# Delta keys kept unnormalised in a hybrid decoder layer: the norm moves into beta and the values

## The chip, the cores and the metric

The kernel runs on one core of one Trainium2 chip. The metric is the device time of one execution in microseconds (us); the time of a kernel is the median of its runs. Engines are named as in the profile: PE is TensorE (matmul), PEld its loading of weights, DVE VectorE, ACT ScalarE, POOL GpSimd, SP SyncE, on whose queue all transfers here are issued.

## The reference

One decoder layer with 512 tokens (T) and 2048 channels (D): a sliding-window attention branch and a gated DeltaNet branch run side by side on the same normalised input, and a gated sum of both goes through an output projection. What matters here is the delta branch. Its keys, per head of 128 channels, are convolved, passed through SiLU, and divided by their norm:

```python
dq = jnp.repeat(l2_norm(dq.reshape(B, T, DN_K_HEADS, DN_HEAD_K)), rep, axis=2)
dk = jnp.repeat(l2_norm(dk.reshape(B, T, DN_K_HEADS, DN_HEAD_K)), rep, axis=2)
beta = jax.nn.sigmoid(db.astype(f32))
...
k_beta = k * beta[..., None]
v_beta = v * beta[..., None]
L = jnp.where(strict, jnp.einsum('bhncd,bhnsd->bhncs', k_beta, k) * decay, 0.0)
t_inv = lax.linalg.triangular_solve(eye + L, jnp.broadcast_to(eye, L.shape),
                                    left_side=True, lower=True, unit_diagonal=True)
u = t_inv @ v_beta
w = t_inv @ (k_beta * jnp.exp(g)[..., None])
```

There are 16 key heads and 32 value heads; two value heads share a key head. Chunks have 64 tokens. A scan over chunks then uses k, u, w and the decays.

## The kernel before

**Products.** Every large product is computed in fp32 precision by three passes: a weight is split into a high part (whi, a cast on ACT, L61) and a low part (wlo, a subtraction on DVE, L62), and `mm3` (L270 to L275) issues whi with hh, whi with hl, and wlo with hh, where hh and hl are the split activations. A `channel_tile` (L290 to L303) makes 128 output channels for all 512 tokens: 16 steps of three 128x512 matmuls, 48 in all, called products in this document. The weights come in loads of 1 MB ("raw", L215) on SP, two of them held at a time, and are split in halves of 1024 columns, three of which are held.

**Order of the work.** The channel tiles follow each other without a pause, and all other work is woven in between. After every second step of a tile, that is after six products, `pump()` advances the side work: each generator that is alive (`go`) counts down and runs to its next `yield n`, which makes it sleep n pumps; the triangular solve is paced by a budget for each pump (`paced`, 0.36), and another sideline runs at a rate of its own. That gives the order in which the program is written. When it is built, a scheduler orders the instructions of each engine once more by its own idea of when each becomes ready, so a change of a few pumps can shift neighbours on every engine. On the chip each engine then keeps its fixed order.

**Stages.** After the startup come the keys (`delta_keys`, about 125 to 445 us of the profile: 16 key tiles mixed with merge gates), the attention (to about 1015 us: four groups of eight tiles, each opened by the transposition pss, L1418, with scores S, L1451, the softmax tile sm, its transposition pP, L320, the output O, L1514, and a sum of squares qss, L1412), the heads (`delta_heads`, to about 2130 us: 16 groups of five tiles q, v, v, z, z), then the output products of the delta branch and the end of the layer.

**keys()** (L729 to L772) is the side work of one key tile: convolution (`conv`), ptk (four 128x128 transpositions on PE to token order, in one PSUM bank of `ptp`, which has two), the sums of squares (ACT, L778), after three pumps the loads of the decay rows E on SP (L783) and the inverse root rk on DVE (L69 to L74), after four more k = ptk · rk as four activations on ACT (L745) and the masks on E (POOL, L788), after four more ptkT (four transpositions back, of the normalised k) with its copy to kT (ACT, L753), the store of k and eight exponentials on E (ACT, L794), after two more pkk = kT · kT (four matmuls), the store of kT and the product of E and pkk (DVE, L763), and after two more the stores of E to lt_d and lab_d.

**solve()** (L796 to L848) waits for eight key tiles, loads the 64 x 64 triangles and beta, multiplies the triangles by −beta (nbet, L815), inverts them step by step on DVE (L823 and L831, each step a product and a sum of up to 128x1024) and multiplies the inverse by beta. It runs twice, the first time in the keys and attention stages, the second beside the heads.

**heads**: `queries()` (L883 and on) loads kT and k, the decays and the inverses, transposes q (ptq), and makes the chunk matrices; `neg_beta` scales one block of them. `values()` (L866 to L878) convolves v, transposes it (ptv) and copies it to vt (ACT, L877). `scan()` walks four blocks of 128 tokens: it multiplies k and kT with the state S, makes pv and pod, and ends with ms (L1023), an inverse root (L69 to L74, tiles roy and rot), the scaled output osb (L1030), its transposition pto, and its product with the gate z.

Of the kernel before, what the change touches and what calls it, by code (L numbers as in the profile page):

```python
# [45 lines left out]
class Layer:  # L46
# [524 lines left out]
    def gates(self, sp):  # L571

        nc, a, dnc = self.nc, self.a, self.dnc
        pt = self.ptp
        bd = sp.tile([P, NTB, 2 * VH], F32, name="bd")
        S = [P, NTB, VH]
# [11 lines left out]
        nc.vector.tensor_tensor(out=bd, in0=pb[:, :, 2 * VH :], in1=bd, op=ALU.add)  # L588
        beta = self.beta = dnc.tile(S, F32, name="beta")
        e = sp.tile(S, F32, name="ge")  # L590
# [138 lines left out]
    def keys(self, wk, g, ps):  # L729

        nc = self.nc
        y = wk.tile([P, T], F32, tag="y", name="y", bufs=3)
        yield from self.conv(wk, ps, 16 + g, y)
        yield 2
        pt = self.ptp.tile([P, T], F32, tag="tp", name="ptk")
        self.transpose4(pt, lambda c: y[:, c * P : (c + 1) * P])
        ss = self.sumsq(wk, pt)
        yield 3
        E = [self.decay_load(wk, 2 * g + e) for e in range(2)]
        nc.vector.tensor_scalar(out=ss, in0=ss, scalar1=EPS, scalar2=None, op0=ALU.add)  # L740
        rk = self.rsqrt(wk, ss, NTB, "rk")
        yield 4
        k = wk.tile([P, NTB, P], F32, tag="k", name="k")
        for c in range(NTB):
            nc.scalar.activation(k[:, c, :], pt[:, c * P : (c + 1) * P], AF.Copy, scale=rk[:, c : c + 1])  # L745
        for e in range(2):
            self.decay_mask(E[e])
        yield 4
        pt = self.ptp.tile([P, T], F32, tag="tp", name="ptkT")
        self.transpose4(pt, lambda c: k[:, c, :])  # L750
        nc.sync.dma_start(out=self.k_d[g], in_=k.rearrange("p c d -> p (c d)"))
        kT = wk.tile([P, T], F32, tag="kT", name="kT")
        nc.scalar.copy(out=kT, in_=pt)  # L753
        for e in range(2):
# [3 lines left out]
        for c in range(NTB):  # L758
            sl = slice(c * P, (c + 1) * P)
            nc.tensor.matmul(pk[:, c, :], lhsT=kT[:, sl], rhs=kT[:, sl], start=True, stop=True)  # L760
        nc.sync.dma_start(out=self.kT_d[g], in_=kT)
        for e in range(2):
# [33 lines left out]
    def solve(self, wk, b, eng):  # L796
# [16 lines left out]
        nb = wk.tile([P, HD], F32, tag="nbet", name="nbet", bufs=1)  # L813
        self.behind(eng.tensor_scalar(out=nb, in0=bet, scalar1=-1.0, scalar2=None, op0=ALU.mult))
# [54 lines left out]
    def values(self, wk, g, e, ps, st):  # L869
# [6 lines left out]
        vt = wk.tile([P, NTB, P], F32, tag="vt", name="vt", bufs=3)  # L876
        nc.scalar.copy(out=vt.rearrange("p c d -> p (c d)"), in_=pt)  # L877
        st[f"v{e}"] = vt  # L878
# [928 lines left out]
```

## Time and profile before

| what | us |
|---|---|
| three runs | 2845.51, 2839.72, 2842.66 |
| their median | 2842.66 |
| span of the profiled execution, first to last instruction | 2839.0 |
| PE busy in it | 2806.5 |
| PE busy of 175.00 in the keys' first part (125 to 300) | 173.21 |
| PE busy of 145.00 in their second part (300 to 445) | 145.00 |
| PE busy of 570.00 in the attention (445 to 1015) | 567.64 |
| PE busy of 435.00 in the heads' first part (1015 to 1450) | 430.19 |
| PE busy of 680.00 in the heads' second part (1450 to 2130) | 679.69 |

The profiled execution's own time is not listed apart; its span lies 3.7 us below the median of the runs. In the rows of a timeline a duration runs to the modelled end of a pipelined matmul, so the next one starts before it; what an instruction costs PE is read from one start to the next. A row "A <- B" in the waits says that A's engine stood until B had ended. In the rows of groups the numbers behind the bar are the busy us, the mean ns of one instruction, and the idle time before them with what ended it. In a table of windows each engine has its busy us and number of instructions, in the order PE, PEld, DVE, ACT, POOL, and then come the granted clock of TensorE as a share of full speed, the busy share of the DMA engines, and GB/s.

### The profile page before, as it was taken

How to read it: one execution, taken by the hardware profiler on the slowest of the kernel's cores; microseconds unless marked ns; L12 is line 12 of the kernel's file. 1: busy time of each engine (PE TensorE's matmuls, PEld its weight loads, DVE VectorE, ACT ScalarE, POOL GpSimd, SP SyncE). 2: the span in 40 equal slices, each digit the busy share in tenths (PEclk: the TensorE clock that was granted, in tenths of full speed). 3: DMA queues.
4: the chain of work that ended last, by engine and by line, in shares of the span. 5: the costliest groups of instructions: out<-in, count | busy, mean ns of one | idle time of the engine just before them, and what ended most of it. 6: DMA issues, size and time to landing. Idle time of an engine off the chain costs nothing.

```text
span 2839.0 us, 38354 instructions
## 1 busy us (share of the span) xinstructions
PE 2806.5 (99%) x14152; PEld 2283.3 (80%) x14152; DVE 1944.8 (69%) x3185; ACT 1207.1 (43%) x2476; POOL 146.0 (5%) x124
## 2 busy tenths in 40 slices
PE   8999999999999999999999999999999999999999
PEld 6788888877776788888888888888888888878887
DVE  7866876867758667778766666666656766664676
ACT  5555443244544443333434333333334454432443
POOL 0010000100000010000001000000000000000000
PEclk9999999999999999999999999999999999999999
DMA  9877764322243253356777667677647886885684
GB/s 402 335 246 230 257 218 139 110 91 91 82 135 119 101 168 110 117 201 219 247 255 262 235 224 242 210 239 238 231 167 252 289 314 240 302 273 180 242 318 168
DMA packets 228512, 603.25 MB, mean 212 GB/s; under 512 B 76354, under 2 KB 102594, under 8 KB 188002
## 3 DMA queue, kind: packets, MB, share of 16 engines
q1 hardware_dynamic: 228324, 600.80, 62.1%
q8 instruction: 111, 1.82, 0.3%
q14 instruction: 77, 0.63, 0.1%
HBM read 480.32 MB, written 118.17 MB: 211 GB/s over the span
## 4 chain that ended last, share of the span: by engine, by line
PE 91%; DMA 3%; DVE 3%; ACT 1%; issue 1%; SPq 0%; POOL 0%; DVEq 0%; ACTq 0%; POOLq 0%
PE mm L273 22%; PE mm L275 21%; PE mm L274 21%; PE m L274 5%; PE m L273 5%; PE m L275 5%; PE pod L1000 1%; PE O L1514 1%; PE pv L981 1%; DVE wlo L62 1%; PE pod L999 1%; PE pod L996 1%; PE pp L971 1%; PE S L1451 1%; DMA wa<-in_w_ada_ss 1%
## 5 line engine op out<-in xcount | busy, mean ns | idle before, releaser
L273 PE MATMUL mm<-hh,whi 128*128 128x512 f32 x2784 | 1130.4, 406 | 1.5 <-ACT hh L61 1.5
L275 PE MATMUL mm<-hh,wlo 128*128 128x512 f32 x2784 | 1090.4, 392 | 0.0
L274 PE MATMUL mm<-hl,whi 128*128 128x512 f32 x2784 | 1087.9, 391 | 0.0
L62 DVE TENSOR_TENSOR wlo<-raw,whi 128x1024 fp32r<-128x1024 f32 x516 | 636.9, 1235 | 426.4 <-ACT whi L61 415.4
L61 ACT CAST whi<-raw 128x1024 fp32r<-128x1024 f32 x516 | 541.3, 1050 | 799.9 <-PE mm L274 566.6
L273 PEld LDWEIGHTS mm<-hh,whi 128*128 128x128 f32 x2784 | 524.0, 188 | 117.0 <-issue 14.3
L275 PEld LDWEIGHTS mm<-hh,wlo 128*128 128x128 f32 x2784 | 523.0, 188 | 113.8 <-issue 0.2
L274 PEld LDWEIGHTS mm<-hl,whi 128*128 128x128 f32 x2784 | 524.7, 188 | 100.9 <-issue 1.6
L1246 DVE TENSOR_TENSOR q<-q,q 128x1024 f32<-128x1024 f32 x96 | 124.8, 1300 | 0.0
L794 ACT ACTIVATE E<-E,neg_g 128x128 f32<-128x128 f32 x256 | 81.2, 393 | 92.3 <-POOL E L788 89.6
L831 DVE TENSOR_TENSOR A<-A,atmp 128x62 f32<-128x62 f32 (+30 forms) x124 | 109.5, 883 | 0.6
L823 DVE TENSOR_TENSOR atmp<-A 128x62 f32<-128x62 f32 (+30 forms) x124 | 107.4, 866 | 0.4
L928 POOL TENSOR_TENSOR qe<-qe,yq 128x512 f32<-128x512 f32 x32 | 54.1, 1708 | 923.9 <-DMA qe<-eg_rows 695.9
L1001 ACT COPY osb<-pod 128x256 f32<-128x256 f32 x64 | 23.8, 372 | 152.6 <-PE pod L1000 152.6
L788 POOL TENSOR_SCALAR_AFFINE_SELECT E<-E 128x512 f32<-128x512 f32 x64 | 59.1, 936 | 431.2 <-DMA E<-g_rows 384.5
L983 ACT COPY vn<-pv 128x256 f32<-128x256 f32 x64 | 23.8, 372 | 124.4 <-PE pv L981 124.4
L652 DVE SCALAR_TENSOR_TENSOR yv<-mm,convh,yv 128x511 f32<-128x511 f32 (+2 forms) x96 | 71.2, 742 | 1.1
L988 DVE TENSOR_SCALAR vs<-vn,kd 128x128 f32<-128x128 f32 x96 | 23.1, 283 | 58.3 <-ACT vn L983 58.3
L1482 ACT ACTIVATE sm<-sm,mx,rs 128x128 f32<-128x128 f32 x128 | 61.5, 482 | 3.4 <-DVE mx L1477 2.3
L1011 DVE SCALAR_TENSOR_TENSOR S<-S,egl,pod 128x128 f32<-128x128 f32 x64 | 19.3, 342 | 51.0 <-ACT junk L1004 51.0
L472 DVE SCALAR_TENSOR_TENSOR wa<-wa,silu_cb 128x2048 f32<-128x2048 f32 x22 | 50.1, 2285 | 4.8 <-DMA wa<-in_w_ada_ss 4.8
L657 ACT ACTIVATE th<-yv 128x512 f32<-128x512 f32 x32 | 20.1, 630 | 76.4 <-DVE yv L652 73.7
(444 smaller groups left out, 3678.8 us busy)
## 6 DMA issues: line engine op xcount, KB each, us to landing
raw<-in_w_ch SPq DMA_DIRECT2D x158, 1024.0 KB
wa<-in_w_ada_ss SPq DMA_DIRECT2D x32, 1024.0 KB
q<-in_w_od SPq DMA_DIRECT2D x64, 512.0 KB
g_d<-q SPq DMA_DIRECT2D x64, 512.0 KB
raw<-g_d SPq DMA_DIRECT2D x32, 1024.0 KB
raw<-in_w_od SPq DMA_DIRECT2D x24, 1024.0 KB
gw<-in_w_ada_gate SPq DMA_DIRECT2D x16, 1024.0 KB
E<-g_rows SPq DMA_DIRECT2D x64, 256.0 KB
```

Of the source, the lines that this page charges most:

```text
L61: h = self.nc.scalar.copy(out=hi, in_=src)
L62: l = self.nc.vector.tensor_tensor(out=lo, in0=src, in1=hi.bitcast(F32), op=ALU.subtract)
L273: nc.tensor.matmul(ps, lhsT=wh, rhs=xh, start=first, stop=False)
L274: nc.tensor.matmul(ps, lhsT=wh, rhs=xl, start=False, stop=False)
L275: self.last_mm = nc.tensor.matmul(ps, lhsT=wl, rhs=xh, start=False, stop=last)
L652: nc.vector.scalar_tensor_tensor(out=y[:, s:], in0=ps[:, : T - s], scalar=w[:, j : j + 1], in1=y[:, s:], op0=ALU.mult, op1=ALU.add)
L788: self.last_mask = self.nc.gpsimd.affine_select(out=E, in_=E, pattern=[[0, NTB], [1, P]], compare_op=ALU.is_ge, fill=NEG, base=0, channel_ ...
L794: self.nc.scalar.activation(E[:, c, :], E[:, c, :], AF.Exp, bias=self.neg_g[:, c, h : h + 1])
L823: eng.tensor_tensor(out=t, in0=A[:, m : m + 1, m + 1 :].to_broadcast([P, m, n]), in1=A[:, :m, m : m + 1].to_broadcast([P, m, n]), op=ALU.mult,
L831: self.behind(eng.tensor_tensor(out=A[:, :m, m + 1 :], in0=A[:, :m, m + 1 :], in1=t, op=ALU.add))
L1246: self.behind(nc.vector.tensor_tensor(out=q[f], in0=q[x], in1=q[y], op=ALU.add))
L1482: nc.scalar.activation(t, t, AF.Exp, scale=r[:, h : h + 1], bias=mx[:, h : h + 1], accum_out=den[:, h : h + 1])
```

## The change

With unnormalised keys y, the norm of a token enters twice in L (once by each k). The change keeps y wherever k stood and puts the norm elsewhere: `knorm` = ss · rk (the norm itself, ss being the sum of squares with epsilon, rk its inverse root) scales the values, `inv` = 1/ss scales `neg_beta` and, as rows read back from DRAM, the beta of the solve.

- In `keys()` the convolved y serves as kT: it is stored right behind ptk, and pkk is y · y. The transposition ptkT, the tile kT and its copy are gone. y has four buffers in place of three. k is one copy of 128x512 (ACT) behind the sums of squares in place of four activations with scale rk.
- DVE computes knorm, the reciprocal inv and the scaled neg_beta for each tile. Each eighth tile transposes the inverse sums of eight tiles at once (pinv, 128x64 to 64x128), copies the rows and stores them to `inv_d`.
- From the loads of E to the exponentials there are 2 + 2 pumps in place of 4 + 4.
- `solve()` loads two more small tiles from `inv_d` and multiplies beta by them (128x64).
- `values()` copies ptv by four activations with the scale knorm in place of one copy.

```diff
     def keys(self, wk, g, ps):
...
-        y = wk.tile([P, T], F32, tag="y", name="y", bufs=3)
+        y = wk.tile([P, T], F32, tag="y", name="y", bufs=4)
...
         self.transpose4(pt, lambda c: y[:, c * P : (c + 1) * P])
+        nc.sync.dma_start(out=self.kT_d[g], in_=y)
         ss = self.sumsq(wk, pt)
+        k = wk.tile([P, NTB, P], F32, tag="k", name="k")
+        nc.scalar.copy(out=k.rearrange("p c d -> p (c d)"), in_=pt)
         yield 3
...
         rk = self.rsqrt(wk, ss, NTB, "rk")
-        yield 4
-        k = wk.tile([P, NTB, P], F32, tag="k", name="k")
-        for c in range(NTB):
-            nc.scalar.activation(k[:, c, :], pt[:, c * P : (c + 1) * P], AF.Copy, scale=rk[:, c : c + 1])
+        nc.vector.tensor_tensor(out=self.knorm[:, :, g], in0=ss, in1=rk, op=ALU.mult)
...
+        nc.vector.reciprocal(out=inv, in_=ss.unsqueeze(1).to_broadcast([P, 2, NTB]))
+        nb = self.neg_beta[:, :, 2 * g : 2 * g + 2]
+        nc.vector.tensor_tensor(out=nb, in0=nb, in1=inv.rearrange("p e c -> p c e"), op=ALU.mult)
+        nc.sync.dma_start(out=self.k_d[g], in_=k.rearrange("p c d -> p (c d)"))
+        yield 2
         for e in range(2):
             self.decay_mask(E[e])
-        yield 4
-        pt = self.ptp.tile([P, T], F32, tag="tp", name="ptkT")
-        self.transpose4(pt, lambda c: k[:, c, :])
-        nc.sync.dma_start(out=self.k_d[g], in_=k.rearrange("p c d -> p (c d)"))
-        kT = wk.tile([P, T], F32, tag="kT", name="kT")
-        nc.scalar.copy(out=kT, in_=pt)
+        if g % 8 == 7:
+            pt = self.ptp.tile([P, T], F32, tag="tp", name="pinv")
+            (nc.tensor.transpose(pt[:HD, :P], self.inv[b].rearrange("p h c -> p (h c)"), self.ident))
+            rows = wk.tile([HD, P], F32, tag="invr", name="invr", bufs=1)
+            nc.vector.tensor_copy(out=rows, in_=pt[:HD, :P])
+            half = self.inv_d[16 * b : 16 * b + 16]
+            nc.sync.dma_start(out=half.rearrange("h (c i) -> (h c) i", c=NTB), in_=rows)
+        yield 2
         for e in range(2):
             self.decay_exp(E[e], 2 * g + e)
         yield 2
...
-            nc.tensor.matmul(pk[:, c, :], lhsT=kT[:, sl], rhs=kT[:, sl], start=True, stop=True)
-        nc.sync.dma_start(out=self.kT_d[g], in_=kT)
+            nc.tensor.matmul(pk[:, c, :], lhsT=y[:, sl], rhs=y[:, sl], start=True, stop=True)
...
     def solve(self, wk, b, eng):
...
-            nc.sync.dma_start(
-                out=bet[s],
-                in_=self.b_rows.rearrange("h (c k i) -> k (h c) i", c=4, k=2)[k2, b * HD : (b + 1) * HD, :],
-            )
+            for dst, rows in ((bet, self.b_rows), (nb, self.inv_d)):
+                nc.sync.dma_start(
+                    out=dst[s], in_=rows.rearrange("h (c k i) -> k (h c) i", c=4, k=2)[k2, b * HD : (b + 1) * HD, :]
+                )
         yield 8.0
+        self.behind(eng.tensor_tensor(out=bet, in0=bet, in1=nb, op=ALU.mult))
...
     def values(self, wk, g, e, ps, st):
...
-        nc.scalar.copy(out=vt.rearrange("p c d -> p (c d)"), in_=pt)
+        for c in range(NTB):
+            nc.scalar.activation(vt[:, c, :], pt[:, c * P : (c + 1) * P], AF.Copy, scale=self.knorm[:, c, g : g + 1])
```

The change also moves instructions that it doesn't name. In the fences below each row is one instruction of an engine in its fixed order, with its line, operation, tiles and shape; "x4" stands for four in a row. The lines of the new kernel are up to fifteen higher behind `keys()`.

ACT in the keys stage, around one tile's exponentials (L794), before; th and y are steps of convolutions, whi the weight casts, junk the squares of ptk:

```order
L649 ACTIVATE y<-mm,convh 128x512
L745 ACTIVATE k<-ptk,rky 128x128 x4
L61 CAST whi<-raw 128x1024
L753 COPY kT<-ptkT 128x512
L794 ACTIVATE E<-E,neg_g 128x128 x8
L657 ACTIVATE th<-y 128x512
L61 CAST whi<-raw 128x1024
```

The same engine and stage, now:

```order
L791 ACTIVATE junk,ss<-ptk 128x128 x4
L743 COPY k<-ptk 128x512
L309 ACTIVATE mth<-mm 128x512
L61 CAST whi<-raw 128x1024 x3
L807 ACTIVATE E<-E,neg_g 128x128 x8
L649 ACTIVATE y<-mm,convh 128x512
L61 CAST whi<-raw 128x1024
```

The copy of k stands directly behind the squares, kT's copy is gone, and the exponentials (now L807) stand behind a run of weight casts.

PE in the third attention group, before; mm is a product, S, pP, O and qss belong to the attention:

```order
L275 MATMUL mm<-hh,wlo 128x512
L1451 MATMUL S<-kd_4589,aq 64x192 x3
L320 MATMUL pP<-ident,sm 128x128 x3
L1451 MATMUL S<-kd_4589,aq 64x192 x2
L320 MATMUL pP<-ident,sm 128x128 x5
L1451 MATMUL S<-kd_4589,aq 64x192 x4
L1514 MATMUL O<-pT,vtok_a 64x512
L1451 MATMUL S<-kd_4589,aq 64x192 x2
L1514 MATMUL O<-pT,vtok_a 64x512
L1514 MATMUL O<-pT,vch_4530 64x512 x2
L1451 MATMUL S<-kd_4589,aq 64x192
L1412 MATMUL qss<-qsq,blk 32x128
```

The same transpositions pP, now:

```order
L275 MATMUL mm<-hh,wlo 128x512
L320 MATMUL pP<-ident,sm 128x128
L273 MATMUL mm<-hh,whi 128x512
L320 MATMUL pP<-ident,sm 128x128
L274 MATMUL mm<-hl,whi 128x512
L275 MATMUL mm<-hh,wlo 128x512
L320 MATMUL pP<-ident,sm 128x128
L273 MATMUL mm<-hh,whi 128x512
L320 MATMUL pP<-ident,sm 128x128 x2
L274 MATMUL mm<-hl,whi 128x512
L320 MATMUL pP<-ident,sm 128x128 x3
L275 MATMUL mm<-hh,wlo 128x512
```

Before, the group's S, pP, O and qss follow each other without a product between them; now they stand among products, and the eight pP in five pieces.

DVE in the heads, at the end of the scan that falls into the second window between two ptq (of the three that the prediction speaks of), before; roy and rot are the steps of the inverse root:

```order
L69 TENSOR_SCALAR roy<-ms 128x8
L72 SCALAR_TENSOR_TENSOR rot<-roy 128x8
L73 TENSOR_TENSOR rot<-rot,ms 128x8
L74 SCALAR_TENSOR_TENSOR roy<-rot,roy 128x8
L72 SCALAR_TENSOR_TENSOR rot<-roy 128x8
L73 TENSOR_TENSOR rot<-rot,ms 128x8
L74 SCALAR_TENSOR_TENSOR roy<-rot,roy 128x8
L72 SCALAR_TENSOR_TENSOR rot<-roy 128x8
L73 TENSOR_TENSOR rot<-rot,ms 128x8
L74 SCALAR_TENSOR_TENSOR roy<-rot,roy 128x8
L62 TENSOR_TENSOR wlo<-raw,whi 128x1024
L1030 TENSOR_TENSOR osb<-osb,roy 128x512 x2
```

The last part of the same chain, now:

```order
L652 SCALAR_TENSOR_TENSOR yv<-mm,convh,yv 128x511
L73 TENSOR_TENSOR rot<-rot,ms 128x8
L652 SCALAR_TENSOR_TENSOR yv<-mm,convh,yv 128x510
L74 SCALAR_TENSOR_TENSOR roy<-rot,roy 128x8
L652 SCALAR_TENSOR_TENSOR yv<-mm,convh,yv 128x509
L72 SCALAR_TENSOR_TENSOR rot<-roy 128x8
L845 TENSOR_TENSOR A<-A,atmp 128x38x25
L73 TENSOR_TENSOR rot<-rot,ms 128x8
L659 SCALAR_TENSOR_TENSOR yv<-th,yv 128x512
L74 SCALAR_TENSOR_TENSOR roy<-rot,roy 128x8
L62 TENSOR_TENSOR wlo<-raw,whi 128x1024
L1045 TENSOR_TENSOR osb<-osb,roy 128x512 x2
```

The steps of the inverse root, before in one run, now alternate with steps of a value's convolution (yv) and of the solve (A).

More of the change, by code (lines that the diff above doesn't have):

```diff
@@ L588, in gates @@
         nc.vector.tensor_tensor(out=bd, in0=pb[:, :, 2 * VH :], in1=bd, op=ALU.add)
-        beta = self.beta = dnc.tile(S, F32, name="beta")
+        beta = sp.tile(S, F32, name="beta")
         e = sp.tile(S, F32, name="ge")
@@ L670, in delta_keys @@
         self.k_d = dram.tile([KH, P, T], F32, name="k_d")
+        self.inv_d = dram.tile([VH, T], F32, name="inv_d")
+        self.knorm = self.dnc.tile([P, NTB, KH], F32, name="knorm")
+        self.inv = {}
         self.o_d = dram.tile([VH, P, T], F32, name="o_d")
@@ L741, in keys @@
         rk = self.rsqrt(wk, ss, NTB, "rk")
-        yield 4
-        k = wk.tile([P, NTB, P], F32, tag="k", name="k")
-        for c in range(NTB):
-            nc.scalar.activation(k[:, c, :], pt[:, c * P : (c + 1) * P], AF.Copy, scale=rk[:, c : c + 1])
+        nc.vector.tensor_tensor(out=self.knorm[:, :, g], in0=ss, in1=rk, op=ALU.mult)
+        b, hl = g // 8, 2 * (g % 8)
+        if not hl:
+            self.inv[b] = wk.tile([P, 16, NTB], F32, tag="inv", name="inv")
+        inv = self.inv[b][:, hl : hl + 2, :]
+        nc.vector.reciprocal(out=inv, in_=ss.unsqueeze(1).to_broadcast([P, 2, NTB]))
[3 more added lines that the diff above has]
+        yield 2
         for e in range(2):
             self.decay_mask(E[e])
-        yield 4
-        pt = self.ptp.tile([P, T], F32, tag="tp", name="ptkT")
-        self.transpose4(pt, lambda c: k[:, c, :])
-        nc.sync.dma_start(out=self.k_d[g], in_=k.rearrange("p c d -> p (c d)"))
-        kT = wk.tile([P, T], F32, tag="kT", name="kT")
-        nc.scalar.copy(out=kT, in_=pt)
+        if g % 8 == 7:
[6 more added lines that the diff above has]
+        yield 2
         for e in range(2):
@@ L802, in solve @@
         bet = wk.tile([P, HD], F32, tag="bet", name="bet", bufs=1)
+        nb = wk.tile([P, HD], F32, tag="nbet", name="nbet", bufs=1)
         for k2 in range(2):
@@ L807, in solve @@
             )
-            nc.sync.dma_start(
-                out=bet[s],
-                in_=self.b_rows.rearrange("h (c k i) -> k (h c) i", c=4, k=2)[k2, b * HD : (b + 1) * HD, :],
-            )
+            for dst, rows in ((bet, self.b_rows), (nb, self.inv_d)):
+                nc.sync.dma_start(
+                    out=dst[s], in_=rows.rearrange("h (c k i) -> k (h c) i", c=4, k=2)[k2, b * HD : (b + 1) * HD, :]
+                )
         yield 8.0
-        nb = wk.tile([P, HD], F32, tag="nbet", name="nbet", bufs=1)
+        self.behind(eng.tensor_tensor(out=bet, in0=bet, in1=nb, op=ALU.mult))
         self.behind(eng.tensor_scalar(out=nb, in0=bet, scalar1=-1.0, scalar2=None, op0=ALU.mult))
```

## The prediction

> **What bounds the kernel now.** I read the page first: the span, the busy times and the chain of work that ended last.
>
> ```profile
> span 2839.0 us, 38354 instructions
> PE 2806.5 (99%) x14152; PEld 2283.3 (80%) x14152; DVE 1944.8 (69%) x3185; ACT 1207.1 (43%) x2476; POOL 146.0 (5%) x124
> PE 91%; DMA 3%; DVE 3%; ACT 1%; issue 1%; SPq 0%; POOL 0%; DVEq 0%; ACTq 0%; POOLq 0%
> ```
>
> TensorE (PE) is busy 99% of the span and carries 91% of the chain. Work saved on ACT, DVE or a queue is worth nothing by itself; PE's instructions count, and the few places where PE stands. The waits of PE (us in total, times, longest) name those:
>
> ```profile
> PE rowb L503 <- DVE xnT L418: 6.8, 1, 6.8
> ...
> PE pto L320 <- DVE osb L1030: 2.4, 2, 2.0
> ...
> PE pP L320 <- DVE sm L1490: 2.3, 3, 1.7
> PE ptv L320 <- DVE yv L659: 1.6, 1, 1.6
> ```
>
> The first lies in the startup, which the change leaves alone. The other three lie in stages whose code the change hardly touches, but whose order of instructions it moves. So the sum has two parts: PE's work in the keys stage, and stalls and clumps that a shifted order takes away or makes. The profiled execution's span is 2839.0 us; the runs' median, 2842.66, lies 3.7 us above it, and I add that at the end. This kernel's time can be told from no change at about 0.2%, 5.7 us.
>
> **PE in the keys stage.** The second transposition, ptkT, as PE's timeline shows it (start, duration, instruction), once for all 16 tiles:
>
> ```profile
> 164.80 0.39 PE L275 MATMUL mm<-hh,wlo 128*128 128x512 f32 x1
> 165.03 0.60 PE L320 MATMUL ptkT<-ident,k 128*128 128x128 f32 x4
> 165.38 0.49 PE L273 MATMUL mm<-hh,whi 128*128 128x512 f32 x1
> 165.70 0.39 PE L274 MATMUL mm<-hl,whi 128*128 128x512 f32 x1
> ```
>
> And the places at which PE stood before ptk, the first transposition (the bracket gives the wait):
>
> ```profile
> 209.30 0.39 PE L275 MATMUL mm<-hh,wlo 128*128 128x512 f32 x1
> ...
> 209.98 0.39 PE L275 MATMUL mm<-hh,wlo 128*128 128x512 f32 x1
> 211.25 0.66 PE L320 MATMUL ptk<-ident,y 128*128 128x128 f32 x4 [0.87 <-ACT k L745]
> ...
> 223.84 0.39 PE L275 MATMUL mm<-hh,wlo 128*128 128x512 f32 x1
> 224.36 0.63 PE L320 MATMUL ptk<-ident,y 128*128 128x128 f32 x4
> ```
>
> Durations overlap, so I go by starts. Three products take 209.98 − 209.30 = 0.68 us, 0.227 each. From 164.80 to 165.70 stand two products and the four transpositions: 0.90 − 2 × 0.227 = 0.45 us a group, of which 0.35 is the four themselves (165.03 to 165.38) and 0.10 the edges to and from the products. Sixteen groups go: **−7.2 us** (6 to 8). Two pinv transpositions come, each a lone one: 0.35/4 + 0.10 = 0.19, together **+0.4** (0.2 to 0.9). The four pkk products keep shape and number and only read y in place of kT.
>
> [...]
>
> In the second fence ptk waits for its PSUM bank, held until ACT has made k out of it, and k needs the inverse root from DVE. PE lost 211.25 − 209.98 − 0.23 = 1.04 and 224.36 − 223.84 − 0.23 = 0.29 us. In the new code k is a plain copy right behind the squares, so the bank comes free without DVE: **−1.3** (0 to −1.3).
>
> **The exponentials, four pumps earlier.** What can cost something is the row of pauses in keys(): from the load of E to its exponentials there were 4 + 4 pumps, and there are 2 + 2. A pump is six products, 1.36 us, so the plan falls from 10.9 to 5.4 us. E's load on SP, the masks on POOL and the exponentials on ACT, for a quick and a slow tile, and ACT's waits for the masks in the stage:
>
> ```profile
> 190.51 0.33 SPq L783 DMA_DIRECT2D E<-g_rows  x1
> 195.51 0.63 POOL L788 TENSOR_SCALAR_AFFINE_SELECT E<-E 128x512 f32<-128x512 f32 x1 [10.02 <-DMA E<-g_rows]
> 281.94 1.21 SPq L783 DMA_DIRECT2D E<-g_rows  x2
> 291.25 1.77 POOL L788 TENSOR_SCALAR_AFFINE_SELECT E<-E 128x512 f32<-128x512 f32 x2 [27.80 <-DMA E<-g_rows]
> 294.67 2.45 ACT L794 ACTIVATE E<-E,neg_g 128x128 f32<-128x128 f32 x8
> ```
>
> ```profile
> ACT E L794 <- POOL E L788: 27.1, 13, 3.3
> ```
>
> The load lands 5.0 to 9.3 us after its issue, so the masks finish 5.6 to 11.1 us after it, and the new plan wants the exponentials at 5.4. ACT works in order, so it will stand longer before them, with weight casts queued behind, then wlo on DVE, then PE. The cover is the lead of the split weights. The tightest place of the stage:
>
> ```profile
> 343.51 1.22 DVE L62 TENSOR_TENSOR wlo<-raw,whi 128x1024 fp32r<-128x1024 f32 x1
> ```
>
> ```profile
> 348.47 0.40 PE L275 MATMUL mm<-hh,wlo 128*128 128x512 f32 x1
> ```
>
> Even there wlo was done 3.7 us before PE read it, and the new order on ACT puts two or three casts ahead of the exponentials. I take **+1.0** (0 to +6, the upper end a stop of 2 us at three tiles).
>
> **Off the path.** k costs ACT less, the values more:
>
> ```profile
> L745 ACT ACTIVATE k<-ptk,rky 128x128 f32<-128x128 f32 x64 | 18.3, 367 | 24.5 <-DVE rky L74 24.5
> L877 ACT COPY vt<-ptv 128x512 f32<-128x512 f32 x32 | 18.6, 580 | 0.4 <-PE ptv L320 0.4
> ```
>
> In the values four activations stand for one copy: by themselves 4 × 0.37 = 1.47 against 0.58 us, at most 0.9 × 32 = 28 us more on an engine that is 43% busy. The scan reads them 18 products (4.1 us) or more behind ptv, which hides it; without that cover it would be 0.9 us a tile. DVE's reciprocal and two small products per tile (a small operation like the ms below takes 0.16 us), the product of beta in the solve and the two more small loads on SP stand beside PE with leads of several us: 0. SP issues the k_d and kT_d stores earlier and nothing waits for them before the heads.
>
> **The order in the attention.** The solve starts four pumps earlier, and with it its loads on SP. In the third attention group the order of before has a run of S, pP, O and qss with no product between. The transposition pss opens each group:
>
> ```profile
> 667.41 0.60 PE L1418 MATMUL pss<-ident,ssb 128*128 128x128 f32 x4
> 774.75 0.49 PE L1418 MATMUL pss<-ident,ssb 128*128 128x128 f32 x3
> 891.11 0.60 PE L1418 MATMUL pss<-ident,ssb 128*128 128x128 f32 x4
> ```
>
> ```profile
> 865.02 0.72 PE L320 MATMUL pP<-ident,sm 128*128 128x128 f32 x3 [1.68 <-DVE sm L1490]
> ```
>
> ```profile
> 866.00:868.00 2.00, 2.00 (x17) 1.02 (x13) 1.86 (x5) 0.59 (x1) 0.00 (x0) 0.60 0.00 0
> 868.00:870.00 2.00, 2.00 (x8) 0.38 (x6) 1.17 (x3) 1.89 (x4) 0.00 (x0) 0.54 0.08 16
> ```
>
> The groups took 107.34 and 116.36 us: 9.0 too many in the second, made of the 1.68 us wait, of a granted clock of 0.60 and 0.54 for 4 us (third column from the end), and of work that ran without products to fill it. The new order spreads it: pP stands in five pieces among products, of which I charge four edges of 0.10 and 1.2 us for a wait on sm that may stay. 9.0 − 0.4 − 1.2: **−7.4** (−5 to −9).
>
> **The order in the heads.** ptq marks a head group; four of them in a row, then PE's wait for pto and DVE's work before it:
>
> ```profile
> 1116.22 0.60 PE L320 MATMUL ptq<-ident,yq 128*128 128x128 f32 x4
> 1185.24 0.60 PE L320 MATMUL ptq<-ident,yq 128*128 128x128 f32 x4
> 1252.48 0.60 PE L320 MATMUL ptq<-ident,yq 128*128 128x128 f32 x4
> 1324.01 0.60 PE L320 MATMUL ptq<-ident,yq 128*128 128x128 f32 x4
> ```
>
> ```profile
> 1264.83 0.66 PE L320 MATMUL pto<-ident,osb 128*128 128x128 f32 x4 [2.00 <-DVE osb L1030]
> ```
>
> ```profile
> 1253.36 0.16 DVE L1023 SCALAR_TENSOR_TENSOR ms<-osq,epsq 128x4 f32<-128x4 f32 x1 [1.24 <-ACT junk L1004]
> ...
> 1263.03 2.78 DVE L1030 TENSOR_TENSOR osb<-osb,roy 128x512 f32<-128x512 f32 x2
> ```
>
> The windows take 69.02, 67.24 and 71.53 us; 67.24 is the undisturbed one. The first loses 1.78 (the ptv wait of the list above, behind a step of the solve on DVE), the third 4.29: on DVE the chain from ms to osb is mixed with the solve, the convolution and wlo and takes 9.7 us. The solve runs on DVE through these windows, so four pumps shift which one it hits. In the new order the first has no step of the solve in the way (−1.8), the second gets the mixed chain, with pto one to seven products later than in the third of before, so about 1 us less: +3.3; the third keeps the mixed chain, but starts it earlier: I leave 1.4 (−2.9). Together **−1.4** (−6, all gone, to +4, both at 4.3 with the first one's 1.8 gone or kept).
>
> **Sum.** −7.2 + 0.4 − 1.3 + 1.0 − 7.4 − 1.4 = −15.9 us: a span of 2823.1, a time of **2826.8 us**.
>
> **Rivals.** *Only the work counts.* The clump and the mixed chains come from the order, and another order may have as many elsewhere. Then −7.2 + 0.4 − 1.3 = −8.1: 2834.6, still faster. For it: three waits of the list of PE lie at places that only the order made. Against: outside the places named, PE's new order is the old one, four pumps shifted around the solve. 0.20.
>
> *Within 0.2%.* The same, and the exponentials cost 4 us: 2838.6, against a limit of 2837.0. 0.12.
>
> *Slower: the exponentials block ACT.* Place: the eight exponentials of each key tile. With the slow landing the masks finish at 11.1 us and ACT stands 11.1 − 5.4 = 5.7 us; if every tile had only the 3.7 us of lead of the tightest, PE would stop 2.0 us. At the 13 tiles that wait for masks already that is 26 us: −15.9 − 1.0 + 26 = +9.1, 2851.8. It decides from a landing of 9.3 − 2.0 = 7.3 us on, if the lead is 3.7. For it: the slow tile's rows, and ACT's 27.1 us. Against: the quick tile, and PE waits for no weights in this stage now. [...] 0.07.
>
> That the change doesn't do what it says is excluded: ptkT is gone from PE's order.
>
> **Chances and range.** My forecast 0.61, the first rival 0.20, the second 0.12, the third 0.07. Faster 0.81, same 0.12, slower 0.07. The range takes in the forecast's bounds (the attention at −9 and the heads at −6 give 2820.6, without the 1.0 for the exponentials 2819.6) and reaches over the first rival to the limit of the second: 2820 to 2838.
>
> **What would show it.** In the profile after: no ptkT; between two key tiles' ends 48 products and about 0.45 us less; no wait of ptk on k. pss at 107 to 109 us apart three times. ptq windows near 67.2, 70.5 and 68.6. ACT's wait on the masks above 27 us, with no wait of PE's products on whi or wlo. The forecast is wrong if products in the keys wait for weights, if a pss interval is again above 112 us, or if the list of PE's waits has a new row of several us.

## The result and the profile after

The changed kernel takes 2824.32 us (median of five runs, 2821.99 to 2829.09), the kernel before, run beside it again, 2839.72 us (2836.82 to 2845.51). The ratio is 0.9948, with a 95% interval from 0.9936 to 0.9961: 15 us less, between 11 and 18. The forecast was 2826.8.

The page of the profile after, the same three lines as before:

```profile
span 2820.5 us, 38292 instructions
PE 2790.0 (99%) x14090; PEld 2271.8 (81%) x14090; DVE 1947.0 (69%) x3237; ACT 1207.8 (43%) x2508; POOL 145.1 (5%) x124
PE 90%; DMA 4%; DVE 3%; ACT 1%; issue 1%; SPq 0%; POOL 0%; DVEq 0%; POOLq 0%; ACTq 0%
```

PE is the bound as before, with 16.5 us less of busy time; DVE and ACT have as much as before, since what the keys save on ACT the values spend. The waits of PE after:

```profile
PE rowb L503 <- DVE xnT L418: 6.8, 1, 6.8
...
PE pto L320 <- DVE osb L1045: 3.0, 2, 2.2
PE m L274 <- DVE wlo L62: 2.9, 4, 1.8
```

Of the three waits that the prediction named, ptv (0.9 us) and pP (1.2) are down, and pto has stayed; the wait of the last products (m, behind the heads) has grown from 1.3 us. Then the landmarks on PE's timeline, pss and ptq:

```profile
656.40 0.60 PE L1433 MATMUL pss<-ident,ssb 128*128 128x128 f32 x4
763.75 0.60 PE L1433 MATMUL pss<-ident,ssb 128*128 128x128 f32 x4
872.79 0.60 PE L1433 MATMUL pss<-ident,ssb 128*128 128x128 f32 x4
...
1097.63 0.60 PE L320 MATMUL ptq<-ident,yq 128*128 128x128 f32 x4
1164.90 0.60 PE L320 MATMUL ptq<-ident,yq 128*128 128x128 f32 x4
1234.57 0.60 PE L320 MATMUL ptq<-ident,yq 128*128 128x128 f32 x4
1302.83 0.60 PE L320 MATMUL ptq<-ident,yq 128*128 128x128 f32 x4
```

The distances are 107.35 and 109.04 us in the attention (107.34 and 116.36 before), and 67.27, 69.67 and 68.26 in the heads (69.02, 67.24, 71.53 before; the forecast had 67.2, 70.5 and 68.6).

For the comparison by stage I take the starts of the products, 48 to a tile. "Keys" are the first 28 tiles from the first product of the stage on; "group 3" is the eight attention tiles that the prediction calls the third group; w1 to w3 are the three windows between ptq, counted by their five tiles, w6 is the third window behind w3 (the seventh head group). All in us, from one profiled execution each; the runs from the third on are the experiments. The runs of the kernel before beside them had medians of 2838.6 to 2841.5, and the ratios are to those.

| run | keys | group 3 | w1 | w2 | w3 | w6 | span | median | ratio to before, 95% |
|---|---|---|---|---|---|---|---|---|---|
| before | 344.1 | 116.1 | 69.0 | 67.2 | 71.5 | 67.4 | 2839.0 | 2839.7 | |
| after | 334.5 | 109.1 | 67.3 | 69.7 | 68.3 | 67.2 | 2820.5 | 2824.3 | 0.9936 to 0.9961 |
| back | 344.2 | 109.3 | 67.2 | 74.7 | 68.3 | 67.2 | 2836.0 | 2837.8 | 0.9985 to 1.0002 |
| twice | 348.2 | 109.1 | 67.4 | 71.3 | 68.4 | 67.2 | 2835.2 | 2837.0 | 0.9981 to 0.9998 |
| late | 341.2 | 115.5 | 69.0 | 67.2 | 71.6 | 67.4 | 2835.4 | 2839.5 | 0.9990 to 1.0007 |
| short | 349.6 | 108.1 | 67.4 | 73.6 | 68.4 | 67.2 | 2838.2 | 2840.5 | 0.9998 to 1.0016 |
| plain_v | 335.6 | 109.1 | 67.3 | 71.2 | 68.3 | 67.2 | 2821.4 | 2823.2 | 0.9933 to 0.9959 |
| pause1 | 344.9 | 111.2 | 68.5 | 71.4 | 68.0 | 68.6 | 2835.0 | 2837.0 | 0.9986 to 1.0004 |
| late1 | 335.4 | 117.7 | 67.2 | 67.3 | 67.3 | 67.2 | 2830.5 | 2830.9 | 0.9950 to 0.9976 |
| rate46 | 335.1 | 107.2 | 67.6 | 67.2 | 67.2 | 67.5 | 2819.4 | 2821.3 | 0.9926 to 0.9950 |
| gap4 | 343.8 | 112.1 | 67.2 | 67.9 | 67.2 | 70.7 | 2830.2 | 2832.1 | 0.9960 to 0.9983 |
| agap6 | 335.7 | 109.5 | 67.2 | 68.8 | 67.2 | 70.3 | 2822.1 | 2825.4 | 0.9932 to 0.9957 |
| r50gap4 | 335.8 | 109.0 | 67.2 | 67.2 | 67.2 | 67.7 | 2823.3 | 2822.1 | 0.9925 to 0.9950 |
| pieces | 336.8 | 108.8 | 69.1 | 67.2 | 67.6 | 70.8 | 2825.7 | 2824.1 | 0.9932 to 0.9960 |

Of the 18.5 us between the two profiled spans, the keys hold 9.6, group 3 7.1, and all head groups together 1.9. The startup was 1.4 shorter, the stages behind the heads 2.6 longer and the last part 0.9 shorter, in code that the change leaves alone; these move by as much between other runs too (the startup lies between 121.9 and 123.5 us in the 14 profiles). Some 3.4 us of the 18.5 are a matter of the granted clock (an estimate, last section): behind the startup the profile before has two stretches of 3.4 us at 0.50, one in group 3 and one in w3, and the profile after has none before its last 3 us.

### The profile page after: what moved, and what is told of

Read it like the earlier page. It is cut to its first block, busy times and chain, and to the rows that moved or that the text cites. A ratio compares the mean times of both kernels' runs of the same rounds, so it can differ in the third digit from the quotient of the medians.

```text
span 2820.5 us, 38292 instructions
## 1 busy us (share of the span) xinstructions
PE 2790.0 (99%) x14090; PEld 2271.8 (81%) x14090; DVE 1947.0 (69%) x3237; ACT 1207.8 (43%) x2508; POOL 145.1 (5%) x124
## 4 chain that ended last, share of the span: by engine, by line
PE 90%; DMA 4%; DVE 3%; ACT 1%; issue 1%; SPq 0%; POOL 0%; DVEq 0%; POOLq 0%; ACTq 0%
PE mm L273 22%; PE mm L275 22%; PE mm L274 21%; PE m L274 4%; PE m L275 4%; PE m L273 4%; PE pv L996 1%; PE pod L1015 1%; PE O L1529 1%; DMA E<-g_rows 1%; PE pod L1014 1%; PE pod L1011 1%; PE pp L986 1%; PE S L1466 1%; DVE wlo L62 1%
## 5 line engine op out<-in xcount | busy, mean ns | idle before, releaser
L1261 DVE TENSOR_TENSOR q<-q,q 128x1024 f32<-128x1024 f32 x96 | 123.5, 1286 | 0.0
L807 ACT ACTIVATE E<-E,neg_g 128x128 f32<-128x128 f32 x256 | 81.0, 390 | 82.3 <-POOL E L801 80.4
L837 DVE TENSOR_TENSOR atmp<-A 128x62 f32<-128x62 f32 (+30 forms) x124 | 109.0, 879 | 0.5
L801 POOL TENSOR_SCALAR_AFFINE_SELECT E<-E 128x512 f32<-128x512 f32 x64 | 63.3, 1002 | 416.3 <-DMA E<-g_rows 344.2
L652 DVE SCALAR_TENSOR_TENSOR yv<-mm,convh,yv 128x511 f32<-128x511 f32 (+2 forms) x96 | 71.3, 743 | 1.1
L1003 DVE TENSOR_SCALAR vs<-vn,kd 128x128 f32<-128x128 f32 x96 | 23.2, 284 | 54.3 <-ACT vn L998 54.3
```

The lines of the kernel that those rows point to most:

```text
L652: nc.vector.scalar_tensor_tensor(out=y[:, s:], in0=ps[:, : T - s], scalar=w[:, j : j + 1], in1=y[:, s:], op0=ALU.mult, op1=ALU.add)
L801: self.last_mask = self.nc.gpsimd.affine_select(out=E, in_=E, pattern=[[0, NTB], [1, P]], compare_op=ALU.is_ge, fill=NEG, base=0, channel_ ...
L807: self.nc.scalar.activation(E[:, c, :], E[:, c, :], AF.Exp, bias=self.neg_g[:, c, h : h + 1])
L837: eng.tensor_tensor(out=t, in0=A[:, m : m + 1, m + 1 :].to_broadcast([P, m, n]), in1=A[:, :m, m : m + 1].to_broadcast([P, m, n]), op=ALU.mult,
L1261: self.behind(nc.vector.tensor_tensor(out=q[f], in0=q[x], in1=q[y], op=ALU.add))
```

## Experiments

**back and twice: the price of four transpositions.** The first puts ptkT and its copy back into the changed kernel, read by nothing:

```diff
+        pt = self.ptp.tile([P, T], F32, tag="tp", name="ptkT")
+        self.transpose4(pt, lambda c: k[:, c, :])
+        kT = wk.tile([P, T], F32, tag="kT", name="kT")
+        nc.scalar.copy(out=kT, in_=pt)
         for e in range(2):
             self.decay_exp(E[e], 2 * g + e)
```

> The changed kernel with the second transposition and its copy to kT put back for each key tile, both read by nothing; the order of the rest is that of the changed kernel. Theory (16 groups at 0.45 us): the keys stage is 7.2 us longer, attention and heads unchanged, 2831.5 us. Rival one (a group costs more than the 0.45 us read at one place, as the measured 9.7 us of the keys suggest): 8 to 9 us, 2833 us. Rival two (the transpositions fit beside other work): 2824 us.

The second issues ptk twice:

```diff
         self.transpose4(pt, lambda c: y[:, c * P : (c + 1) * P])
...
+        self.transpose4(pt, lambda c: y[:, c * P : (c + 1) * P])
         ss = self.sumsq(wk, pt)
```

> The changed kernel with the first transposition ptk issued twice, eight 128x128 transpositions in one run for each key tile. Theory (a group is 0.35 us of four transpositions and 0.10 us of edges to the products): 16 x 0.35 = 5.6 us more, 2830 us. Rival (every group of four costs 0.45 us wherever it stands): 7.2 us more, 2831.5 us.

Putting ptkT back costs the keys 9.7 us, all that the change had gained there (344.2 against 344.1 before), and the second rival, that it is hidden, is out. The group itself takes 0.46 us at each of its 16 places in this run, 7.4 in all; the other 2.3 us stand mostly at three single tiles, which take 0.5 to 0.7 us more than that. In the run with eight transpositions at a time PE's timeline reads:

```profile
173.26 0.39 PE L275 MATMUL mm<-hh,wlo 128*128 128x512 f32 x1
173.50 1.03 PE L320 MATMUL ptk<-ident,y 128*128 128x128 f32 x8
174.29 0.48 PE L273 MATMUL mm<-hh,whi 128*128 128x512 f32 x1
174.60 0.40 PE L274 MATMUL mm<-hl,whi 128*128 128x512 f32 x1
```

From 173.26 to 174.60 stand two products and eight transpositions: 1.34 − 0.45 = 0.89 us, so the second four cost 0.43 and not the 0.35 that I expected, and the edges are worth only 0.03. Sixteen times 0.43 is 6.9 us; the keys of this run are 13.7 longer, most of the rest being stops of PE before ptk, 3.6 us of it at one tile. Both runs lose in w2 as well, where PE has the same order as after the change. In back, PE waits 5.7 us for osb there, in place of 2.2. In twice it waits 2.2 us as after the change, and w2 takes 71.3 us, as in plain_v (71.2), where the products behind the same wait run at a granted clock of 0.50 (last section). So the work is priced well, but the same order of PE can lose microseconds more from one run to another.

**late and short: the start of the solve.** One keeps the change and starts the solve when it started before; the other keeps the kernel before and starts it earlier, through shorter pauses:

```diff
 late, against the changed kernel
+        yield 4
         self.keys_done.append(g)
 short, against the kernel before
-        yield 4
+        yield 2
         k = wk.tile([P, NTB, P], F32, tag="k", name="k")
...
-        yield 4
+        yield 2
         pt = self.ptp.tile([P, T], F32, tag="tp", name="ptkT")
```

> The changed kernel, but each key tile is reported as done four pumps later, so that the solve starts where it started before; the keys themselves keep the change. Theory (two parts, work and order): the order in the attention and the heads becomes that of before, so the third attention group is back at about 116 us between two pss (109 now) and the ptq windows at 69.0, 67.2 and 71.5 us (67.3, 69.7 and 68.3 now), the keys stage keeps its 9.7 us of gain, and the time is 2824.3 + 7.1 + 1.9 = 2833 us. Rival (the stalls went because the keys and their norm are lighter, not because of the start of the solve): attention and heads stay as after the change, 2824 us.

> The kernel before, with only the two pauses of the keys shortened from 4 and 4 to 2 and 2 pumps: ptkT, the normalised k and all else stay. Theory (order): the solve starts four pumps earlier and the attention and the heads take the order of the changed kernel: 109 us between the pss, ptq windows 67.3, 69.7 and 68.3; with ptkT still there 2839.7 - 9 = 2831 us, plus what the nearer exponentials cost in this kernel, whose k waits for the inverse root and holds its PSUM bank (0 to 4 us). Rival (all of the gain is work on PE in the keys and in the values): 2840 us and windows as before.

The attention and w1 to w3 follow the start of the solve: group 3 is at 115.5 in late and 108.1 in short, and w1 to w3 in late are those of before within 0.1 us. The rival of both, that the lighter keys or values made those stages quicker, is out. But both are 6 to 10 us slower than I expected, and the loss lies mostly in the keys: late has 341.2 where I had 334.5, and short has 349.6 against 344.1 before, with 4.0 us of waits of ptkT for k at four places; w2 of short is another 3.9 us longer than after the change. In late the stop comes as the first solve starts. ACT, DVE and PE at that place:

```profile
287.89 1.03 ACT L61 CAST whi<-raw 128x1024 fp32r<-128x1024 f32 x1
295.09 0.28 ACT L792 ACTIVATE junk<-ptk 128x128 f32<-128x128 f32 x1 [6.17 <-PE ptk L320]
...
295.35 1.04 ACT L61 CAST whi<-raw 128x1024 fp32r<-128x1024 f32 x1
296.29 2.44 ACT L808 ACTIVATE E<-E,neg_g 128x128 f32<-128x128 f32 x8
```

```profile
292.14 4.43 DVE L830 TENSOR_TENSOR A<-A,nbet 128x4096 f32<-128x4096 f32 x1
297.65 0.69 DVE L776 TENSOR_TENSOR E<-pkk,E 128x512 f32<-128x512 f32 x1 [1.09 <-ACT E L808]
298.26 1.22 DVE L62 TENSOR_TENSOR wlo<-raw,whi 128x1024 fp32r<-128x1024 f32 x1
```

```profile
299.53 0.79 PE L275 MATMUL mm<-hh,wlo 128*128 128x512 f32 x1 [2.63 <-DVE wlo L62]
```

A weight cast stands on ACT behind a square of ptk that PE has not made yet (6.17 us of idle time), wlo stands on DVE behind a product with E that waits for the exponentials, and PE waits 2.63 us for wlo. In these rows each engine does only what its fixed order says. That tile took 3.8 us longer than after the change, another 1.9. So the changed kernel with the old start is not told from the kernel before (0.9990 to 1.0007): the work taken off PE is there, but the stalls of one unlucky order eat most of it.

**plain_v: the scaling of the values.** The four activations become one copy again, and the kernel leaves out the scaling of the values by the norm:

```diff
-        for c in range(NTB):
-            nc.scalar.activation(vt[:, c, :], pt[:, c * P : (c + 1) * P], AF.Copy, scale=self.knorm[:, c, g : g + 1])
+        nc.scalar.copy(out=vt.rearrange("p c d -> p (c d)"), in_=pt)
```

> The changed kernel with the values copied by one activation and without their scaling by the norm (this part of the computation is left out); PE's order is that of the changed kernel. Theory (the four activations lie beside PE's products): head windows and time as after the change, 2824 us, each undisturbed ptq window at 67.2 us. Rival (the longer copies cost on the path, up to 0.9 us for each of 32 tiles): up to 28 us less, with windows at 65.5 us.

The median is 1.1 us lower, inside the spread of either kernel's runs, and the undisturbed windows stay at 67.24. The values' scaling is hidden. (w2 is 1.6 us longer than after the change, with the same order of PE and the same wait; the last section comes back to it.)

**pause1: the exponentials nearer still.**

```diff
-        yield 2
+        yield 1
         for e in range(2):
             self.decay_mask(E[e])
...
-        yield 2
+        yield 1
         for e in range(2):
             self.decay_exp(E[e], 2 * g + e)
```

> The changed kernel with pauses of 1 and 1 pumps in place of 2 and 2 between the loads of E and the exponentials, so that the plan wants them 2.7 us after the load. Theory (the lead of the split weights covers ACT's wait, and order decides the rest): no wait of PE's products on whi or wlo, keys within 1 us of 334.5 us, apart from places at which the order of ptk on PE is another (666 in place of 678 products), where the run called late lost 3.8 us; time 2822 to 2830. Rival (ACT, working in order, stands before the exponentials and the weights come late): the keys lose 2 us or more at each of several tiles, 10 us or more in all, 2835 us or more.

The keys lose 10.4 us, as much as the rival has it, but not by its trigger. From the 16th tile on, each pair of tiles takes 23.2 us as after the change, although the exponentials are now planned 2.7 us behind the load. The whole loss lies in the first 14 tiles, 8.7 us of it in the last three of them, during and just after the load of the first solve's triangles (2 MB). SP's queue, POOL and ACT there:

```profile
255.11 0.54 SPq L819 DMA_DIRECT2D A<-lt_d  x1
...
257.60 0.90 SPq L796 DMA_DIRECT2D E<-g_rows  x2
...
282.94 0.61 SPq L215 DMA_DIRECT2D raw<-in_w_ch  x1
```

```profile
270.67 1.22 POOL L801 TENSOR_SCALAR_AFFINE_SELECT E<-E 128x512 f32<-128x512 f32 x2 [23.80 <-DMA E<-g_rows]
```

```profile
271.43 0.28 ACT L791 ACTIVATE junk<-ptk 128x128 f32<-128x128 f32 x1 [6.19 <-PE ptk L320]
...
275.25 2.45 ACT L807 ACTIVATE E<-E,neg_g 128x128 f32<-128x128 f32 x8
...
289.09 1.04 ACT L61 CAST whi<-raw 128x1024 fp32r<-128x1024 f32 x1 [1.01 <-DMA raw<-in_w_ch]
```

E lands 13.1 us after its issue behind A's load (at most 10.8 at the other key tiles of this run), while the DMA engines are busy throughout (share 0.98 to 1.03 from 255 to 270 us). But that is not what held ACT. Both masks are done at 271.89, and the exponentials start 3.4 us later without a wait: as in late, ACT had stood before the squares of ptk, and casts stand between these and the exponentials. PE waits 1.39 us for wlo behind that. Then E's stores stand on SP until 278.30, waiting for the product with E (on DVE from 277.59), the weight load behind them is issued only at 282.94, ACT's cast waits for it, and PE waits 2.83 us for whi. So the rival's chain is there, from ACT to PE, but its trigger, a late mask, is not; the nearness of the exponentials costs nothing from the 16th tile on.

**late1 and gap4: what the attention lost.** Two ways to take the run of attention work without products out of the order:

```diff
 late1, against the changed kernel
+        yield 1
         self.keys_done.append(g)
 gap4, against the kernel before, at the end of solve()
                 out=self.ts_d[b, k2].rearrange("h c j i -> (h c) (j i)"), in_=A[s].rearrange("u j i -> u (j i)")
             )
+        yield 4.0
```

> The changed kernel with each key tile reported as done one pump later. The order has no clump in the attention, and of the mixed chains on DVE in the heads one is left (third scan, 7.6 us of work between ms and osb) where the changed kernel has three (9.7, 7.5, 7.5). Theory (order): second ptq window 67.2 in place of 69.7, third about 68.3, third attention group 107 to 109, keys as after the change, 334 to 336 us; time 2821 to 2824. Rival (small shifts bring as many stalls elsewhere as they remove, as in the run called late): keys at 338 or more and time 2828 to 2835.

> The kernel before, with nothing changed but a pause of 4 us of the solve's budget (11 pumps) between the stores of the first half's inverse and the load of the second half's triangles, so that on SP a weight load stands between them instead of waiting behind both. The order then has no run of attention work without products, and the chains on DVE in the heads are short (3 to 4 us of work). Theory (the weight load behind the solve's load cost the 9 us in the attention, the mixed chains the 6 us in the heads): third attention group 107 to 108 us (116.1 before), ptq windows 67.2 to 67.6 (69.0, 67.2, 71.5 before), keys as before at 344 us, time about 2839.5 - 8.5 - 5.5 = 2825.5 us, with none of the change in it. Rival (the group waits for weights in any order, as in the run called late1): the third group at 113 or more and time 2833 or more.

late1 has no such run and yet 117.7 us in group 3: there my theory fell. PE's waits of late1 between 820 and 900 us, what stood on DVE and ACT at that place, and SP's queue of before, after, late1 and gap4, one fence each:

```profile
PE mm L275 <- DVE wlo L62: 3.4, 1, 3.4
PE mm L273 <- ACT whi L61: 1.7, 1, 1.7
```

```profile
853.75 4.41 DVE L830 TENSOR_TENSOR A<-A,nbet 128x4096 f32<-128x4096 f32 x1
853.87 1.03 ACT L61 CAST whi<-raw 128x1024 fp32r<-128x1024 f32 x1
...
858.68 2.28 DVE L62 TENSOR_TENSOR wlo<-raw,whi 128x1024 fp32r<-128x1024 f32 x1
```

```profile
844.92 1.10 SPq L805 DMA_DIRECT2D A<-lt_d  x2
...
848.23 0.38 SPq L215 DMA_DIRECT2D raw<-in_w_ch  x1
```

```profile
819.38 1.17 SPq L215 DMA_DIRECT2D raw<-in_w_ch  x1
...
823.36 1.08 SPq L819 DMA_DIRECT2D A<-lt_d  x2
```

```profile
831.00 1.10 SPq L820 DMA_DIRECT2D A<-lt_d  x2
...
834.31 0.38 SPq L215 DMA_DIRECT2D raw<-in_w_ch  x1
```

```profile
842.17 0.39 SPq L215 DMA_DIRECT2D raw<-in_w_ch  x1
...
843.18 0.50 SPq L805 DMA_DIRECT2D A<-lt_d  x1
```

Where the weight load (raw) stands behind the load of A for the second solve, which waits until the first half's stores have left A's buffer (2.8 us of SP's waits, before and after the change alike), group 3 takes 115 to 118 us: in before, late and late1. In the nine other runs that load A at this place it stands ahead, and the group takes 108 to 112: after and gap4 among them. So the run of attention work was the filling of a gap, not its cause; in late1 the gap is there without the filling: PE waits 5.1 us, and its granted clock is 0.50 for about 10 us.

That the load's place is the cause of the gap is argued and not shown. In late1 the DMA engines are idle from 850 to 854 us (share 0.00), so the weights had landed when ACT cast them at 853.87; the cast stood behind the softmax, and wlo behind the solve's product over A (4.41 us). And in r50gap4 a weight load stands behind A as well, at 660.44 us, and no group takes more than 109.5. How much of the loss is the load and how much the order of ACT and DVE stays open.

gap4 shows the other side: with the order alone, and nothing of the change, the kernel before gains 0.3% (0.9960 to 0.9983), about 8 us (I expected 14: keys as before, w1 and w3 at 67.2, but 3.3 us lost at one tile of group 3 and 3.5 in w6).

**agap6 and pieces: what is left there.** A pause at the same place in the changed kernel, of 6.0 in place of 4.0, and then with the solve's two products over the whole of A cut in four:

```diff
 agap6, against the changed kernel, at the end of solve()
+        yield 6.0
 pieces, against agap6; the product with bet alike
-        self.behind(eng.tensor_tensor(out=A, in0=A, in1=nb.unsqueeze(1).to_broadcast([P, HD, HD]), op=ALU.mult))
+        for q in range(4):
+            if q:
+                yield 0.1
+            j = slice(16 * q, 16 * q + 16)
+            self.behind(eng.tensor_tensor(out=A[:, j], in0=A[:, j], in1=nb.unsqueeze(1).to_broadcast([P, 16, HD]), op=ALU.mult))
```

> The changed kernel with a pause of 6 us of the solve's budget at the same place, after the stores of the first half's inverse. Order: a weight load between the stores and the load, chains on DVE in the heads 3 to 4 us. Theory: third attention group 107.3 (109.1 after the change), ptq windows 67.2 to 67.6, keys as after the change, 334.5 to 336; time 2819 to 2821, and 6 to 10 us below the kernel before with its own pause, which is then the worth of the work taken off PE. Rival (another place pays, as in the keys of the run called late): keys at 340 or a group longer by 4 us or more, 2826 us or more.

> The run called agap6 (the changed kernel with a pause between the halves of the solve), with the solve's two products over the whole of A, 4.4 us each on DVE, cut into four pieces of 1.1 us with short pauses between them. Theory (what is left in the third attention group and in the seventh head window is DVE held for 4.4 us by one instruction, with the softmax and a value's convolution queued behind it): third attention group 107.2 to 107.5 (109.5 in agap6), seventh head window 67.2 to 67.6 (70.3), time 2825.4 - 5.3 = 2820 us, or 2818.5 if the third window (68.8) goes to 67.2 too. Rival (the losses come from the transfers of A or from the number of steps, not from the length of one instruction): both places within 0.5 us of agap6, 2825 us.

gap4 and agap6 have both a pause there and differ by the change and by the pause's length: 335.7 against 343.8 in the keys, 8.1 us, and 6.7 us between the medians. That is the nearest that these runs come to the worth of the change without the order; behind the keys the two orders still differ (w2, w6 and group 3 by 0.4 to 2.6 us). What both lose at one tile of group 3, 3.3 us in gap4 and 2.3 in agap6, comes with one instruction, here in agap6 on DVE, with PE's wait behind it:

```profile
879.37 4.42 DVE L829 TENSOR_TENSOR A<-A,nbet 128x4096 f32<-128x4096 f32 x1
883.71 0.42 DVE L1476 TENSOR_TENSOR sm<-S,mask 128x256 f32<-128x256 f32 x1
```

```profile
884.18 0.71 PE L1462 MATMUL S<-kd,aq 64*128 64x128 f32 x4 [1.59 <-DVE sm L1476]
```

Cut in four, that tile is back at 14.8 us (17.1 in agap6), as expected; but the next one has 1.5 us more, and in w6 three of the four pieces ran one behind the other, held another small copy for PE, and the loss there is as large as before (70.8); w1 has 69.1 where agap6 has 67.2. The median is 1.3 us lower, where I expected 5, which the spread of the runs doesn't tell from nothing. So it is half shown: the length of the instruction was the cause in group 3; in w6 cutting it was no remedy.

**rate46 and r50gap4: the solve out of the heads.** The solve is paced faster, so that it ends before the heads begin to share DVE with it:

```diff
-            self.solves = self.paced(self.solve_all(), 0.36)
+            self.solves = self.paced(self.solve_all(), 0.46)
```

r50gap4 has 0.50 and a pause of 4.0 behind the stores.

> The changed kernel with the solve paced at 0.46 of a budget for each pump in place of 0.36: its steps are written closer together and end before the heads need DVE. The order has no clump in the attention and no mixed chain in any scan. Theory (order): all ptq windows at 67.2 to 67.4 us (3.5 to 5 us less than after the change), third attention group at 107 to 109; in the keys ptk stands at 666 products as in the run called late, so they may lose 3 to 7 us there; time 2820 to 2828. Rival (the denser solve takes DVE from wlo and the softmax in the attention): attention groups longer than 107.4 us by 1 us or more each, 2830 us or more.

> The changed kernel with the solve paced at 0.50 in place of 0.36 and a pause of 4 us of its budget between its halves: the solve ends before the heads, where it met DVE's chains. Theory: attention groups at 107.2 to 107.4 three times, every ptq window at 67.2 to 67.6, keys 334.5 to 336; 2816 to 2820 us, the fastest of all. Rival (the denser solve collides in the attention, as the second full group of the run called rate46 did with 111.1): one group at 110 to 112, 2820 to 2824 us.

The windows w1 to w3 and w6 are at 67.2 to 67.7 in both, and no chain from ms to osb takes more than 4.8 us there (up to 9.7 in the kernel before and 11.0 after the change): the mixed chains were the loss in the heads. The price moves to the attention, as the rivals said: 111.1 us in the second group of rate46, 109.0 to 109.5 in the three groups of r50gap4, which is therefore slower than the 2816 to 2820 us that I expected. rate46 has the lowest median, 2821.3, 3 us below the changed kernel; the intervals to the kernel before overlap, so whether it beats the changed kernel stays open.

## Why the prediction was right

The time, its sign and its parts came out. Step by step:

- *ptkT, −7.2:* measured the same way at every place, from the last product before to the fourth after, 15 groups cost 0.46 or 0.47 us each in the profile before (one more is split in three and one), so about 7.4 us, and 7.4 when put back. Right, 0.2 low. The two pinv cost 0.13 us each, 0.3 in place of 0.4. The run twice has 0.89 us for eight, 111 ns each, where the row's 0.45 us for four is 113.
- *ptk's waits, −1.3:* gone, 1.4 us. The keys gained 9.6 us; these three terms make 8.5, and 8.1 is what gap4 and agap6 show. The last 1 to 1.5 us lie at single tiles that differ from run to run.
- *The exponentials, +1.0:* nothing in the changed kernel: no product waits for weights in the keys. One sign did not come: ACT's wait for the masks in this stage was to rise above 27 us, and it fell to 23.5. It was not safe, though: late and pause1 show the chain that the third rival described (ACT in its order, casts behind, wlo, PE), set off in both by the squares of ptk; that a late mask sets it off, no run shows. In these rows ACT keeps to its order: in late the cast behind the waiting square starts only after it (at 295.35, the square at 295.09), and ACT stood 6.17 us.
- *The attention, −7.4:* 7.1. The size was right and the cause half: I named the run of work without products, and late1 showed that this was only the filling of a gap. The gap goes with the weight load's place behind the solve's load on SP; what makes it is not shown to the end.
- *The heads, −1.4:* 1.9, and the three windows within 0.9 us of the forecast. rate46 shows the cause. w2 lost 2.4 in place of 3.3; the wait was as long as that in w3 of before, but no slow products came behind it. That was luck: in plain_v, with the same order of PE in w2 and the same wait, they came, and w2 lost 4.0, about as much as in twice (below).

There is more luck in it. The first rival, that stalls of a shifted order come back elsewhere, had 0.20; it is what happened in late, back, twice and pause1, where the keys lost 2 to 10 us more than their work. That the order of the changed kernel has none of them there could be seen only by running it.

## What to carry to other kernels

Here, with one engine busy 99% of the time, the work taken off it counted about in full (8.5 us priced from one start to the next in the trace, 8.1 us between the keys of gap4 and agap6); but the gain measured is that plus what the shifted order does, and the two were of about equal size (8 us from the pair gap4 and agap6, 7 to 9 in the attention and the heads). To tell them apart, put a pause that changes the order into both kernels and compare; the two pauses should be alike, which those of this pair were not quite. And where a run of work without products is seen in an order, take it away before calling it the cause: in late1 the run was gone and the loss stayed.

## What the runs showed of the hardware

Two waits of PE cost 1.4 and 2 times their length: 3.8 us at the tile of the 2.63 us wait in late, 3.5 us in w6 of pieces with a wait of 1.72 us. After both the granted clock fell for about 3 us, to 0.50 and 0.56 (third column from the end, first of late, then of pieces):

```profile
297.00:299.50 2.50, 0.00 (x0) 0.00 (x0) 1.85 (x3) 2.50 (x10) 0.00 (x0) 0.97 0.00 0
299.50:302.50 3.00, 2.97 (x7) 2.39 (x8) 3.00 (x7) 2.01 (x6) 0.00 (x0) 0.50 0.42 99
302.50:305.00 2.50, 2.50 (x11) 2.01 (x11) 2.50 (x10) 0.00 (x0) 0.00 (x0) 0.95 0.90 216
```

```profile
1460.50:1463.50 3.00, 1.28 (x19) 1.09 (x19) 3.00 (x5) 0.96 (x1) 0.00 (x0) 1.00 1.21 240
1463.50:1466.50 3.00, 3.00 (x10) 2.33 (x9) 3.00 (x6) 0.63 (x1) 0.00 (x0) 0.56 0.93 229
```

It doesn't follow each wait. After the change, PE waited 2.25 us for osb and went on at full rate (a granted clock of 1.00 from 1172 to 1184 us):

```profile
1177.50 0.66 PE L320 MATMUL pto<-ident,osb 128*128 128x128 f32 x4 [2.25 <-DVE osb L1045]
1177.91 0.48 PE L274 MATMUL mm<-hl,whi 128*128 128x512 f32 x1
1178.23 0.60 PE L320 MATMUL pto<-ident,osb 128*128 128x128 f32 x4
```

In plain_v the same order of PE in the same window met a wait of the same length, and the clock fell:

```profile
1179.62 0.66 PE L320 MATMUL pto<-ident,osb 128*128 128x128 f32 x4 [2.24 <-DVE osb L1044]
```

```profile
1178.00:1181.00 3.00, 1.38 (x10) 1.36 (x11) 3.00 (x4) 0.29 (x2) 0.00 (x0) 0.97 0.32 55
1181.00:1184.00 3.00, 3.00 (x8) 2.32 (x8) 1.40 (x3) 0.00 (x0) 0.00 (x0) 0.50 0.96 391
```

That is why w2 lost 2.4 us after the change and 4.0 in plain_v. w3 of before lost 4.3, with waits of 2.0 and 0.4 us and a granted clock of 0.50 from 1266 to 1269 us. The profile before has such a fall in group 3, too, at 866 us. A fall is worth about 1.7 us (an estimate from the two rows of 866 to 870 us in the prediction: 2 × 0.40 + 2 × 0.46), so two of them make the 3.4 us named above. What decides whether the clock falls, these runs don't show.
